# Hybrid residual block on one core: fill work ahead of the recurrence, transposes spread along the attention heads, two paired projection units turned into four single gates

## The chip, the core and the metric

The kernel runs on 1 core of one Trainium2 chip. Its time is the device time of one execution in microseconds. The median of 3 runs is 1808.64 us (1808.52 to 1810.89). All arithmetic is 32-bit: a large matrix product is done as three passes over operands that were split into a rounded high part and the rest (`h` and `l`), so that "a matmul of the program" is a group of three on TensorE at lines L115, L116 and L117 (helper `mm3`).

## The reference

One layer of a streaming encoder on x (1024 tokens x 1024 channels) and 256 memory tokens:

```
h = rmsnorm(x);  z = h @ w_in          # 2048 recurrence + 1544 forgetting attention + 512 memory + 3072 gate columns
y_a = gated linear recurrence          # 4 heads, 128x128 state, chunkwise: S = diag(f) S + (1-f) i^T, o = S^T q
y_b = forgetting attention             # 8 heads x 64, softmax(q k^T/8 + F_t - F_s), causal, 128-query blocks, normed q and k
y_c = cross-attention to the memory    # 4 heads x 128
merged = sum over 3 branches of sigmoid(gate_b) * (y_b @ w_b)
x = x + merged @ w_out
x = x + (gelu(conv3(h2 Wa)) * (h2 Wv)) @ w_down ,  h2 = rmsnorm(x)
```

## The kernel before, in words

The program is a chain of stages, and the order of each engine's instructions is fixed when the program is built: a scheduler runs a timeline of the whole program once and writes each engine's instructions down in the order in which that timeline starts them. On the chip every engine works through its list in that order. Three things steer the scheduler. `ahead(gen, 300)` gives a stage's instructions priority. `held(gen, lag)` lets a step of filling work start only behind the instruction that stands `lag` entries back in the list `state["at"]`, to which the recurrence and the attention add their matmuls as they go. `weave` interleaves two generators in proportion to their step counts.

The stages that matter here, with their place in the profiled span:

- 56 to 292 us, the projections that are done in pairs. `dense_unit` takes two 128-channel chunks of the input projection and computes them with seven block products instead of eight (four sums of the right-hand blocks, called T1 to T4, are made once by `differences`; L437 sums the weights). One unit is 7 products x 4 k-blocks x 3 passes = 84 matmuls of 512 columns. There are 11 units: 12 recurrence chunks, 4 memory-query chunks and 6 of the 24 gate chunks (`NPAIR` = 6).
- 292 to 400 us, recurrence values and `NMEM` = 2 single gates, woven with the memory attention. A single gate is `cm_chunk`: 2 halves x 8 k-blocks x 3 passes = 48 matmuls of 512 columns, so two gates take 96.
- 400 to 602 us, four recurrence heads (`hgrn_mix`), each in two halves, woven with a generator `fill` of 33 steps: 16 steps of attention values, one step for the forget-gate cumulative sum (L648 to L659), and 8 steps each of `fox_proj(0)` and `fox_proj(1)`, the query/key projections. A projection step is 8 k-blocks x 3 passes = 24 matmuls of 256 columns. `fox_proj(2)` follows at 602 to 624.
- 624 to 969 us, eight attention heads in four pairs (`fox_attn(p, i)`), woven with `fox_proj(3)` and then with the 12 remaining gates (`NFOX` lists the gates per head). `fox_prep(p)` loads the normed queries and keys of one pair (tile `zl`), transposes them on TensorE (L800, 16 transposes a pair) and spreads each transposed block over tiles `kh`, `kl`, `qa` by ScalarE, VectorE and GpSimd (L805 to L812). The preparation of pair p+1 is issued at the start of the second head of pair p, and its transposes may not start before the last score matmul (L839) of the head before.
- then the branch projections, the output projection, the ConvGLU.

In an attention head one query block goes: scores L838/L839 on TensorE, bias and row maximum on VectorE (L845), exponential on ScalarE (L855), normalising on GpSimd (L857), transposes L869 to L872, split L121/L129, values L881/L882.

## Time and profile before

| what | value |
|---|---|
| median of 3 runs | 1808.64 us |
| the profiled execution | 1810.57 us, its span 1808.8 us, mean granted TensorE clock 0.984 |
| busy share of the span | TensorE 97%, VectorE 67%, ScalarE 45%, GpSimd 17% |
| chain that ended last | TensorE 85%, VectorE 6%, DMA 3%, ScalarE 3% |
| DMA | 256.74 MB, mean 142 GB/s |

"Busy" on TensorE counts a matmul from its start to its modelled end, about 0.39 us for 512 columns, while the next one starts after about 0.23 us. So a price is best read from the starts of neighbouring rows in a timeline, or from a window that holds nothing else, not from the mean duration of a group.

### The profile page before, as it was taken

What the parts mean: (1) busy time and instruction counts of PE and PEld (TensorE: products, weight loads), DVE (VectorE), ACT (ScalarE), POOL (GpSimd) and SP (SyncE); (2) the same over time, 40 slices, a digit from 0 to 9 for tenths busy, and PEclk for the clock granted to TensorE, in tenths of its full rate; (3) what the DMA queues carried; (4) which work ended last, traced back from release to release, by engine and by line L of the source; (5) the groups of instructions that cost most, each with busy time, mean ns of one, the idle gap of its engine ahead of it and who ended that gap; (6) DMA issues with size and microseconds to landing.
All of it is one profiled execution on the core that took longest, in us unless ns stands there. A gap on an engine that the chain in (4) does not pass through costs nothing.

```text
span 1808.8 us, 24826 instructions
## 1 busy us (share of the span) xinstructions
PE 1748.3 (97%) x9021; PEld 1474.3 (82%) x9021; DVE 1207.3 (67%) x2215; ACT 815.9 (45%) x1436; POOL 312.8 (17%) x431
## 2 busy tenths in 40 slices
PE   8999999988989998999999999999999999999999
PEld 6778888967989986877888888878888888888887
DVE  7656665547878566666575665688787777766654
ACT  8634433646565354445452133544444334443332
POOL 1100000314334344333230000021111111100000
PEclk9999999998999998999999999999999999999999
DMA  9533323242221422312147463265545444395682
GB/s 354 175 121 105 97 95 129 83 148 87 94 70 59 165 75 80 108 65 88 55 154 258 146 216 116 98 193 146 150 148 145 130 150 134 111 340 191 227 289 82
DMA packets 97227, 256.74 MB, mean 142 GB/s; under 512 B 10816, under 2 KB 17736, under 8 KB 97104
## 3 DMA queue, kind: packets, MB, share of 16 engines
q1 hardware_dynamic: 77904, 186.46, 29.3%
q0 software_dynamic: 19200, 68.69, 13.1%
q8 instruction: 71, 1.16, 0.3%
q14 instruction: 52, 0.43, 0.1%
HBM read 195.56 MB, written 82.61 MB: 154 GB/s over the span
## 4 chain that ended last, share of the span: by engine, by line
PE 85%; DVE 6%; DMA 3%; ACT 3%; issue 2%; POOL 1%; SPq 0%; DVEq 0%; ACTq 0%; POOLq 0%
PE pp L116 18%; PE pp L117 18%; PE pp L115 18%; PE lg L117 5%; PE lg L115 5%; PE lg L116 5%; PE tr L116 2%; PE tr L115 2%; PE tr L117 2%; PE lg L1001 1%; PE po L882 1%; PE lg L838 1%; PE po L117 1%; PE po L115 1%; PE po L116 1%
## 5 line engine op out<-in xcount | busy, mean ns | idle before, releaser
L121 ACT CAST wh<-s 128x512 fp32r<-128x512 f32 x129 | 77.6, 619 | 174.3 <-PE pp L116 83.8
L115 PE MATMUL pp<-wh,uh 128*128 128x256 f32 (+1 forms) x512 | 149.2, 292 | 0.0
L117 PE MATMUL pp<-wh,ul 128*128 128x256 f32 (+1 forms) x512 | 148.1, 290 | 0.0
L116 PE MATMUL pp<-wl,uh 128*128 128x256 f32 (+1 forms) x512 | 148.1, 290 | 0.0
L115 PE MATMUL pp<-uh,wh 128*128 128x512 f32 x300 | 122.1, 407 | 0.0
L117 PE MATMUL pp<-uh,wl 128*128 128x512 f32 x300 | 121.4, 405 | 0.0
L116 PE MATMUL pp<-ul,wh 128*128 128x512 f32 x300 | 120.4, 401 | 0.0
L121 ACT CAST wh<-rw 128x512 fp32r<-128x512 f32 x99 | 60.3, 619 | 112.5 <-PE pp L116 67.4
L121 ACT CAST wh<-raw 128x1024 fp32r<-128x1024 f32 (+2 forms) x68 | 59.2, 871 | 95.0 <-PE pp L116 86.8
L115 PEld LDWEIGHTS pp<-wh,uh 128*128 128x128 f32 x512 | 99.1, 194 | 0.7
L116 PEld LDWEIGHTS pp<-wl,uh 128*128 128x128 f32 x512 | 98.7, 193 | 0.4
L117 PEld LDWEIGHTS pp<-wh,ul 128*128 128x128 f32 x512 | 98.7, 193 | 0.2
L1308 POOL DMA_DIRECT2D rw<-in_w_up x44 | 24.1, 555 | 428.1 <-ACT sqs L1243 197.4
L121 ACT CAST dwh<-wr 128x1024 fp32r<-128x1024 f32 (+1 forms) x41 | 40.1, 978 | 118.0 <-PE tr L116 38.1
L129 DVE TENSOR_TENSOR wl<-raw,wh 128x1024 fp32r<-128x1024 f32 (+2 forms) x67 | 71.1, 1062 | 23.3 <-ACT wh L121 22.8
L855 ACT ACTIVATE pt<-pt,st 128x128 f32<-128x128 f32 (+3 forms) x64 | 49.7, 777 | 50.1 <-DVE st L852 34.1
L129 DVE TENSOR_TENSOR dwl<-wr,dwh 128x1024 fp32r<-128x1024 f32 (+1 forms) x41 | 46.3, 1130 | 32.5 <-ACT dwh L121 32.5
L115 PEld LDWEIGHTS pp<-uh,wh 128*128 128x128 f32 x300 | 58.3, 194 | 12.0 <-ACT wh L121 0.3
L117 PEld LDWEIGHTS pp<-uh,wl 128*128 128x128 f32 x300 | 57.4, 191 | 12.3
L116 PEld LDWEIGHTS pp<-ul,wh 128*128 128x128 f32 x300 | 57.6, 192 | 11.4
L129 DVE TENSOR_TENSOR pl<-tr,ph 128x512 fp32r<-128x512 f32 (+1 forms) x80 | 49.9, 633 | 20.4 <-ACT ph L121 19.6
L857 POOL TENSOR_SCALAR pt<-pt,st 128x128 f32<-128x128 f32 (+3 forms) x64 | 48.5, 759 | 81.1 <-DVE st L856 55.1
(491 smaller groups left out, 5440.4 us busy)
## 6 DMA issues: line engine op xcount, KB each, us to landing
rw<-in_w_up POOLq DMA_DIRECT2D x44, 512.0 KB, 4.7
sd<-in_w_dn POOLq DMA_DIRECT2D x30, 512.0 KB, 6.0
br<-yd SPq DMA_DIRECT2D x30, 512.0 KB, 4.9
gd<-gt SPq DMA_DIRECT2D x48, 256.0 KB, 2.0
gt<-gd SPq DMA_DIRECT2D x48, 256.0 KB, 2.7
yd<-fc SPq DMA_DIRECT2D x44, 256.0 KB, 2.2
rw<-in_w_pair POOLq DMA_DIRECT2D x20, 512.0 KB, 5.5
wr<-sd SPq DMA_DIRECT2D x20, 512.0 KB, 4.6
```

Source lines behind the costliest of these rows:

```text
L115: PE.matmul(ps, lh, rh, start=first, stop=False, skip_group_check=more)
L116: PE.matmul(ps, lh, rl, start=False, stop=False, skip_group_check=more)
L117: PE.matmul(ps, ll, rh, start=False, stop=last, skip_group_check=more)
L121: return S.copy(out, in_)
L129: return (sub or V).tensor_sub(l, src, h.bitcast(F32))
L838: PE.matmul(ps[:, :w], qa[i][:, tsl], kh[i][:, s0:s0 + w], start=True, stop=False)
L855: S.activation(pt[:, :ns], pt[:, :ns], AF.Exp, bias=st[:, 2:3], accum_out=st[:, 3:4])
L857: late["pool"] = G.tensor_scalar(pt[:, :ns], pt[:, :ns], st[:, 3:4], 0.0, ALU.mult, ALU.add)
L882: late["pv"] = PE.matmul(o, vhl[:, sb, :], pl[:, src], start=False, stop=last)
L1001: mm = PE.matmul(o[:, b * 64:(b + 1) * 64], X[:, b * P:(b + 1) * P], Xq[:, b * bpb:(b + 1) * bpb, :], start=True, stop=True)
L1308: late["raw"] = G.dma_start(raw[:, 2 * i:2 * i + 2, :], src[:, 2 * i:2 * i + 2, :])
```

## The change

- `NPAIR` goes from 6 to 2: 9 paired units instead of 11. The four gates that drop out are computed as single gates in the attention heads: `NFOX` goes from 0,2,2,2,2,2,2,0 to 0,3,2,3,2,3,3,0.
- Five of the 33 steps of `fill` are issued ahead of the first recurrence head, without a hold; each head is then woven with 7 steps (before: 8, 8, 8, 9). The hold's lag is 4 instead of 3, and 10 in the attention heads.
- `fox_prep` becomes a generator: the preparation of the next pair is woven through the second head of each pair instead of standing at its start, with priority; its transposes no longer wait for the score matmul, and its two loads go to the projection's own buffers (`z`, 2 of them) instead of those of the attention weights (`pt`, 4). Three of the eight steps of `fox_proj(3)` come ahead of the first attention head.
- The vector operations that make T2 and T3 are issued behind T1's, without the wait for the first gates.
- The last of the recurrence's eight stores is issued by GpSimd instead of SyncE.

```diff
-NCOVER, NPAIR, NMEM = 2, 6, 2
-NFOX = [0, 2, 2, 2, 2, 2, 2, 0]
+NCOVER, NPAIR, NMEM = 2, 2, 2
+NFOX = [0, 3, 2, 3, 2, 3, 3, 0]
...
-LAG = 3
+LAG, FOX_LAG = 4, 10
...
             V.tensor_sub(b11, b11, b12)
             family_block("T1", k, b11)
+        for t1, b12, b21, b22 in b:
+            V.scalar_tensor_tensor(out=t1, in0=t1, scalar=-1.0, in1=b22, op0=ALU.mult, op1=ALU.subtract)
+            V.tensor_sub(b12, b22, b12)
         yield
         with tc.issue_after(first_gates.ins):
             for k, (t1, b12, b21, b22) in enumerate(b):
-                V.scalar_tensor_tensor(out=t1, in0=t1, scalar=-1.0, in1=b22, op0=ALU.mult, op1=ALU.subtract)
                 family_block("T2", k, t1)
...
             for k, (t2, b12, b21, b22) in enumerate(b):
-                V.tensor_sub(b12, b22, b12)
                 family_block("T3", k, b12)
...
-    def fox_prep(p, after=None):
-        zs = [pf.tile([P, 4, 256], F32, tag="pt", name=f"zl{p}_{n}", bufs=4) for n in range(2)]
+    def fox_prep(p):
+        zs = [z_tile(f"zl{p}_{n}") if p else pf.tile([P, 4, 256], F32, tag="pt", name=f"zl{p}_{n}", bufs=4)
+              for n in range(2)]
...
-                with tc.issue_after(after.ins) if after is not None else nullcontext():
-                    for b in range(4):
-                        PE.transpose(ptr[:, b * P:(b + 1) * P], z[:, b, what * P:(what + 1) * P], ident)
+                for b in range(4):
+                    PE.transpose(ptr[:, b * P:(b + 1) * P], z[:, b, what * P:(what + 1) * P], ident)
...
+                yield
...
-                SP.dma_start(yad[:, h, sl], yo)
+                (SP if h < 3 or n == 0 else G).dma_start(yad[:, h, sl], yo)
...
     fill = chain(fox_values(), fox_proj(0), fox_proj(1))
+    run_all(islice(fill, 5))
     for h in range(4):
-        weave((ahead(hgrn_mix(h), AHEAD), HGRN_STEPS), (held(islice(fill, 8 + (h == 3))), 8))
+        weave((ahead(hgrn_mix(h), AHEAD), HGRN_STEPS), (held(islice(fill, 7)), 7))
...
-    fox_prep(0)
+    run_all(fox_prep(0))
+    rest = fox_proj(3)
+    run_all(islice(rest, 3))
     for p in range(4):
         for i in range(2 if p < 3 else 1):
-            if i:
-                fox_prep(p + 1, fox_sets[p][3])
             count = NFOX[2 * p + i]
             weave((ahead(fox_attn(p, i), AHEAD), FOX_STEPS),
-                  (held(gates_early(count) if p + i else fox_proj(3)), 2 * count if p + i else 8))
+                  (ahead(fox_prep(p + 1), AHEAD) if i else iter(()), 4),
+                  (held(gates_early(count) if p + i else rest, FOX_LAG), 2 * count if p + i else 5))
```

Three places show what the change does to the built order. Lines of the changed kernel lie 1 to 3 below those of the one before (L838 becomes L841, L800 L803, L951 L954).

TensorE where the memory attention ends (`po<-mph`) and the first recurrence head begins (`lg<-qq,kt`). Before:

```order
L117 MATMUL pp<-uh_85,wl 128x512
L115 MATMUL po<-mph,mvh 128x512
L116 MATMUL po<-mpl,mvh 128x512
L117 MATMUL po<-mph,mvl 128x512
L951 MATMUL lg<-qq,kt 128x192 x4
L115 MATMUL pp<-wh,uh_71 128x256
```

Now the same place has 120 matmuls of the attention-value projection (`pp<-wh,uh`, 256 columns) in it; its first rows, where they begin among the last matmuls of the memory attention:

```order
L115 MATMUL po<-mph,mvh 128x512
L115 MATMUL pp<-wh,uh_77 128x256
L116 MATMUL po<-mpl,mvh 128x512
L117 MATMUL po<-mph,mvl 128x512
L115 MATMUL po<-mph,mvh 128x512
L116 MATMUL po<-mpl,mvh 128x512
L117 MATMUL po<-mph,mvl 128x512
L116 MATMUL pp<-wl,uh_77 128x256
L117 MATMUL pp<-wh,ul_78 128x256
```

All five steps stand in TensorE's list before the recurrence's first matmul; 110 of the 120 rows stand behind the last one of the memory attention.

TensorE at the start of the fourth attention head (second head of pair 1), where the transposes of pair 2 (`tr<-ident,zl`) are. Before, the last three groups of four stand close together:

```order
L800 MATMUL tr<-ident,zl_0_7434 128x128 x4
L115 MATMUL pp<-uh_83,wh 128x512
L116 MATMUL pp<-ul_84,wh 128x512
L117 MATMUL pp<-uh_83,wl 128x512
L115 MATMUL pp<-uh_85,wh 128x512
L116 MATMUL pp<-ul_86,wh 128x512
L117 MATMUL pp<-uh_85,wl 128x512
L800 MATMUL tr<-ident,zl_1_7435 128x128 x4
L838 MATMUL lg<-kh_1_6585,qa_1_6587 128x512
L839 MATMUL lg<-kl_1_6589,qa_1_6587 128x512
L800 MATMUL tr<-ident,zl_1_7435 128x128 x4
L869 MATMUL tr<-ident,pt 128x128
```

Now the second group alternates with the attention's own transposes, and the third and fourth come 56 and 119 rows behind it:

```order
L885 MATMUL po<-pl,vhl 128x128
L803 MATMUL tr<-ident,zl_0_7227 128x128
L872 MATMUL tr<-ident,pt 128x128
L803 MATMUL tr<-ident,zl_0_7227 128x128
L873 MATMUL tr<-ident,pt 128x128
L803 MATMUL tr<-ident,zl_0_7227 128x128
L872 MATMUL tr<-ident,pt 128x128
L803 MATMUL tr<-ident,zl_0_7227 128x128
L873 MATMUL tr<-ident,pt 128x128
L117 MATMUL pp<-uh_81,wl 128x512
```

The order also deals the gates differently: in the third and the fifth head (two gates each) it has 103 and 104 gate matmuls, none of them after about two thirds of the head's score matmuls (before: 99 and 89, spread over the whole head); the heads with three gates have 129 to 137.

VectorE around the first gates (`gt<-..,rx`), where the differences for T2 and T3 (`xk<-xk,xk`) are made. Before:

```order
L129 TENSOR_TENSOR T1l<-xk_98,T1h 128x512
L384 TENSOR_TENSOR gt<-lg,rx 128x512 x2
L384 TENSOR_TENSOR gt<-pp,rx 128x512
L129 TENSOR_TENSOR wl<-s_729,wh 128x512
L129 TENSOR_TENSOR wl<-s_735,wh 128x512
L384 TENSOR_TENSOR gt<-po,rx 128x512
L564 SCALAR_TENSOR_TENSOR xk_95<-xk_95,xk_99 128x512
L564 SCALAR_TENSOR_TENSOR xk_96<-xk_96,xk_100 128x512
```

Now:

```order
L129 TENSOR_TENSOR T1l<-xk_98,T1h 128x512
L562 SCALAR_TENSOR_TENSOR xk_96<-xk_96,xk_100 128x512
L562 SCALAR_TENSOR_TENSOR xk_97<-xk_97,xk_101 128x512
L574 SCALAR_TENSOR_TENSOR t4s_516<-xk_95,xk_99 128x512
L562 SCALAR_TENSOR_TENSOR xk_98<-xk_98,xk_102 128x512
L574 SCALAR_TENSOR_TENSOR t4s_517<-xk_96,xk_100 128x512
L574 SCALAR_TENSOR_TENSOR t4ta<-xk_97,xk_101 128x512
L574 SCALAR_TENSOR_TENSOR t4tb<-xk_98,xk_102 128x512
L129 TENSOR_TENSOR wl<-s_733,wh 128x512
L129 TENSOR_TENSOR wl<-s_739,wh 128x512
L384 TENSOR_TENSOR gt<-lg,rx 128x512 x2
L384 TENSOR_TENSOR gt<-pp,rx 128x512
```

All twelve differences, T4's four among them, now stand ahead of the first gates in VectorE's list.

More of the change, by code (lines that the diff above doesn't have):

```diff
@@ L791, in fox_prep @@
         kl = [pf.tile([P, T], F32R, tag=f"kl{i}", name=f"kl{i}_{p}", bufs=1 + i) for i in range(2)]
+        fox_sets[p] = [kh, kl, qa, None, pools["vf"]]
         for n in range(2):
@@ L813, in fox_prep @@
                                                in1=qa[i][a, sl].bitcast(F32), op0=ALU.mult, op1=ALU.subtract)
-        fox_sets[p] = [kh, kl, qa, None, pools["vf"]]
+                yield
     def fox_attn(p, i):
@@ L1045, in hgrn_mix, with finish @@
                     St = Sn
-            def finish(po=po, gz=gz, sl=sl):
+            def finish(po=po, gz=gz, sl=sl, n=n):
                 o2 = ph.tile([P, 4, P], F32, tag="o2", name="o2")
```

## The prediction

> **What bounds the kernel now.** I read the page first, then windows over the stages that the change touches, then timelines at the places where TensorE waits.
>
> ```profile
> PE 1748.3 (97%) x9021; PEld 1474.3 (82%) x9021; DVE 1207.3 (67%) x2215; ACT 815.9 (45%) x1436; POOL 312.8 (17%) x431
> PE 85%; DVE 6%; DMA 3%; ACT 3%; issue 2%; POOL 1%; SPq 0%; DVEq 0%; ACTq 0%; POOLq 0%
> ```
>
> TensorE is 85% of the chain that ended last. The stages differ, and the second view, windows (span, then busy time and count of each engine; the last three columns are the granted clock, the DMA share and GB/s), shows where it is not full:
>
> ```profile
> 241.54:280.60 39.06, 39.06 (x170) 31.55 (x169) 24.07 (x40) 15.75 (x29) 1.05 (x2) 1.00 0.24 81
> 399.50:414.50 15.00, 0.02 (x1) 0.02 (x1) 8.12 (x13) 6.31 (x14) 3.39 (x4) 0.61 0.90 330
> 414.50:435.00 20.50, 19.79 (x144) 19.07 (x145) 15.40 (x32) 15.28 (x39) 7.84 (x9) 0.87 0.07 28
> 500.30:529.30 29.00, 23.93 (x174) 22.48 (x173) 21.75 (x45) 19.16 (x46) 12.13 (x11) 0.88 0.21 65
> 529.30:550.10 20.80, 20.80 (x179) 20.22 (x178) 18.39 (x38) 11.31 (x33) 8.27 (x8) 1.00 0.13 39
> 550.10:571.20 21.10, 21.10 (x181) 20.59 (x180) 19.28 (x39) 13.40 (x33) 10.90 (x10) 1.00 0.24 89
> 624.00:657.00 33.00, 26.31 (x168) 24.14 (x167) 25.80 (x75) 17.57 (x35) 18.02 (x25) 0.84 0.23 78
> 657.00:707.00 50.00, 44.48 (x276) 39.32 (x275) 34.29 (x90) 27.64 (x51) 22.42 (x27) 0.90 0.28 96
> 707.00:745.00 38.00, 36.80 (x202) 30.95 (x201) 21.77 (x74) 16.96 (x36) 10.22 (x17) 1.00 0.23 78
> 745.00:791.50 46.50, 42.57 (x221) 35.41 (x220) 28.78 (x87) 22.89 (x44) 15.59 (x25) 0.93 0.29 101
> 791.50:827.40 35.90, 34.50 (x191) 29.04 (x190) 22.19 (x75) 17.24 (x36) 10.32 (x17) 1.00 0.19 62
> 827.40:873.70 46.30, 42.38 (x220) 35.45 (x219) 28.21 (x87) 22.90 (x44) 15.57 (x25) 0.93 0.27 89
> 873.70:908.80 35.10, 34.47 (x191) 28.98 (x190) 21.41 (x77) 16.62 (x37) 10.30 (x17) 1.00 0.20 64
> sum 319.00, PE 294.97 PEld 251.25 DVE 205.55 ACT 160.14 POOL 113.06; mean PE 36.87 PEld 31.41 DVE 25.69 ACT 20.02 POOL 14.13
> ```
>
> The first row is two paired units: TensorE full, nothing to hide there. The second is an empty gap of 15.00 us ahead of the recurrence. The next four are halves of recurrence heads: full, except 500 to 529. From 624 on come the attention heads, one row each; the sum row has all eight windows (the eighth ends at 943). The second heads of the pairs (745, 827) take 46 us, the first heads (791, 874) 35 to 36.
>
> **The paired units.** Two units go. A full window of two is 39.06 us, so the term is **-39.1 us**, bare TensorE time.
>
> **The four gates.** A gate is 48 matmuls of 512 columns. Three starts in a row:
>
> ```profile
> 760.59 0.39 PE L115 MATMUL pp<-uh,wh 128*128 128x512 f32 x1
> 760.82 0.40 PE L116 MATMUL pp<-ul,wh 128*128 128x512 f32 x1
> 761.05 0.40 PE L117 MATMUL pp<-uh,wl 128*128 128x512 f32 x1
> ```
>
> They lie 0.23 us apart; the two units give 39.06/168 = 0.2325 us. 4 x 48 x 0.2325 = **+44.6 us** of TensorE work. So TensorE has 5.5 us more to do than before, and every microsecond of gain has to come out of time in which it now waits or runs cold. The gates' casts and products on ScalarE and VectorE are hidden: in the window at 745 these have 23 and 29 us of work in 46.5. Without that cover a gate's own vector work (a 1024-wide split and two products) would add under 3 us.
>
> **Slack in the attention heads.** Over the eight windows idle time is 319.00 - 294.97 = 24.0 us; the clock below 1.00 costs at most 0.16 x 33 + 0.10 x 50 + 0.07 x 46.5 + 0.07 x 46.3 = 16.8 us. Together 40.8 us is the most that can be won, 0 the least. What of it the change reaches:
>
> ```profile
> 631.04 0.30 PE L838 MATMUL lg<-kh,qa 128*128 128x128 f32 x1 [3.11 <-DVE qa L812]
> 632.07 0.41 PE L117 MATMUL pp<-wh,ul 128*128 128x256 f32 x1
> 632.29 0.41 PE L115 MATMUL pp<-wh,uh 128*128 128x256 f32 x1
> 769.05 0.63 PE L800 MATMUL tr<-ident,zl 128*128 128x128 f32 x4 [2.47 <-DVE qa L812]
> 770.44 0.30 PE L869 MATMUL tr<-ident,pt 128*128 128x128 f32 x1 [0.76 <-DVE kl L806]
>   DVE qa L812: 6.1, 3
> ```
>
> At 631 TensorE waits 3.11 us for the first pair's preparation and then runs cold (0.21 us between 256-column matmuls that lie 0.119 apart when warm, as quoted further down), some 1.5 us more. With three projection steps ahead that is filled: 5 us. The last row is from the transposes' own view: three waits for VectorE's `qa`, 6.1 us in all, one per preparation of a next pair; 769.05 is one of them. What such a preparation costs in all is the difference between a second and a first head. The gate matmuls in these two windows, by the tiles that they read (`uh`, then `ul`):
>
> ```profile
> 791.50:827.40 35.90, 20.40 (x60) 1.00 0.19 62
> 827.40:873.70 46.30, 24.15 (x69) 0.93 0.27 89
> 791.50:827.40 35.90, 11.69 (x30) 1.00 0.19 62
> 827.40:873.70 46.30, 14.16 (x35) 0.93 0.27 89
> ```
>
> 104 against 90 gate matmuls: 14 x 0.2325 = 3.3 us of the difference of 10.4. The 16 transposes are 16 x 0.09 (the four at 758.75, below, free TensorE after 0.36) = 1.5. The remaining 5.6 us is stall, three times over: 16.8.
>
> ```profile
> 758.75 0.60 PE L800 MATMUL tr<-ident,zl 128*128 128x128 f32 x4
> 759.11 0.48 PE L115 MATMUL pp<-uh,wh 128*128 128x512 f32 x1
> ```
>
> Spreading the groups gives VectorE, ScalarE and GpSimd time between two of them, and the third gate of a second head stands beside them as cover; the 3 loads, 16 transposes and 24 casts of a pair remain. I count 5 + 16.8 = 21.8 as won, 4 us elsewhere from the longer lag (fill may start ten entries behind the attention, so it is at hand when a score waits), and take 6 back: in the third and fifth heads the order has no gate left for the last third, where the attention alone sets the pace. **-20 us**, half of what there is.
>
> **The gap ahead of the recurrence.** It is a chain that no fill was allowed into:
>
> ```profile
> 397.92 1.08 ACT L121 CAST wh<-raw 128x1056 fp32r<-128x1056 f32 x1 [1.99 <-PE pp L116]
> 402.56 6.07 DMA ha<-hd
> 414.51 2.90 PE L951 MATMUL lg<-qq,kt 128*128 128x192 f32 x8 [14.99 <-DVE qq L943]
> 603.20 0.27 PE L115 MATMUL pp<-wh,uh 128*128 128x256 f32 x1
> 603.32 0.28 PE L116 MATMUL pp<-wl,uh 128*128 128x256 f32 x1
> 603.43 0.28 PE L117 MATMUL pp<-wh,ul 128*128 128x256 f32 x1
> ```
>
> The head waits for its own load (6.07 us), logarithm and scan. Five steps are 5 x 24 x 0.119 = 14.3 us and fit. Their weights are there: at 397.92 ScalarE already casts a 1056-wide piece, the second part of the value projection, so the first is ready. The gap itself does not get shorter; the heads do, if TensorE sets their pace: 14.3/8 = 1.8 us a half. In the full halves VectorE has 18.39 of 20.80 and 19.28 of 21.10 us, so 2.4 and 1.8 us is all the room there is, and a bound that close is not reached. I take two thirds: **-9.5 us**. Bounds: 0, if VectorE's chain sets the halves; -17, if all 14.3 come and the lost clock at 414 (0.13 x 20.5 = 2.7) too. The half at 500 with its 5 us of idle moves to another place and stays.
>
> The page "TensorE: Matmul & The Clock Gate" of the Trainium skill (Part 1: The HAM clock gate) says that an idle window of about 3.4 us halves TensorE's clock until it has been busy as long again; by it a filled gap saves about 1.7 us, an estimate from its figures. The clock of 0.61 and 0.87 at the gap agrees in kind; the term above doesn't use it.
>
> **The differences T2 and T3.** In the first unit TensorE waits 0.68 and 0.58 us while VectorE stood idle earlier:
>
> ```profile
> 66.59 1.29 DVE L384 TENSOR_TENSOR gt<-lg,rx 128x512 f32<-128x512 f32 x2 [4.00 <-DMA rx<-rx_d]
> 87.26 0.51 PE L115 MATMUL pp<-T2h,wh 128*128 128x512 f32 x1 [0.68 <-ACT fe L430]
> 91.94 0.50 PE L117 MATMUL lg<-uh,wl 128*128 128x512 f32 x1 [0.58 <-DVE wl L129]
> ```
>
> Four idle microseconds take six of the twelve operations at 0.65 us (two take 1.29 in the first row); the others may push the first gates back by up to 3.9 us, which must not hold a PSUM bank that TensorE wants. **-0.8 us**, between -1.3 and +1.5. The store moved to GpSimd is one issue there, with 18 of 33 us busy: nothing.
>
> **Sum**: -39.1 + 44.6 - 20 - 9.5 - 0.8 = -24.8. The profiled execution took 1810.57 us (span 1808.8 and 1.8 around it), 1.9 above the median of 1808.64. So 1785.8 for such an execution, **1784 us** for the median, 1.4% less. About 0.2% (3.6 us) is what a measurement of this kernel can tell from no change.
>
> **Rivals.** *More is won.* Spread preparation and more fill leave only 11 us of the attention's slack, and the halves shrink by nearly all they can: -39.1 + 44.6 - 30 - 13 - 0.8 = -38.3, 1770 us. For it: first heads, full of gates, keep a clock of 1.00. Against it: the attention's own chain remains.
>
> *The gates only cost what they cost.* The preparation's stall goes elsewhere, nothing of the slack is filled, and VectorE holds the recurrence: -39.1 + 44.6 - 4 - 0.8 = +0.7, 1809 us. For it: VectorE's 92% in the halves. Against: the named waits are TensorE's own, with fill standing behind them.
>
> *Slower.* Ten entries of lag let the fixed order put long blocks of gates ahead of scores: in the second to seventh heads the order has a block of 35 to 61 gate matmuls between two neighbouring pairs of scores (24 at most before). 61 are 14 us in which VectorE, ScalarE and GpSimd run dry, and behind them a last third without cover. At 3 us for each of six heads on top of the case above: 1827 us. It decides as soon as the attention chain alone, from a pair's scores to its values, is longer than the fill left behind it. The same page of the Trainium skill (Part 2: What happens when you issue a matmul) says that matmuls stay in program order and only weight loads move ahead; by it such a block really stands in the way, which 770.44 above, a transpose queued behind the preparation's, bears out in the small.
>
> *The early fill isn't ready.* If a step in the gap waits for its buffers, the head queues behind it and the 9.5 us are gone: 1794 us. The cast at 397.92 speaks against it.
>
> **Chances.** Forecast 0.63, more won 0.15, cost only 0.10, slower 0.07, not ready 0.05. The forecast's own range, with its two slack terms 40% larger or smaller (12 us), is 1772 to 1796. Reaching to the cases on both sides so that about 2 in 10 stay out gives 1764 to 1803. Faster: 0.63 + 0.15 + 0.05 and a third of the third case, 0.86; same 0.06; slower 0.08.
>
> **What would show it.** Right: nine units of 19.5 us; TensorE busy from 399 to 414 with a clock of 1.00; halves of 19 to 20 us; no wait of transposes for `qa`; second heads of 49 to 53 us with three gates at a clock of 0.97 or more; the seventh head at 44 to 47. Wrong: halves still above 20.5 us (VectorE's bound); second heads of 55 or more; idle time in the third and fifth heads' last third above 5 us each; a T2 wait above 2 us.

## The result and the profile after

The changed kernel takes 1793.12 us (median; 1789.67 to 1793.96), the kernel before 1808.58 in the same comparison: a ratio of 0.991 with a 95% interval of 0.9893 to 0.9927. It is faster by 15.5 us, where 24.6 were forecast, and lies in the range. The profiled execution took 1793.35 us, its span 1791.6, 17.2 less than the span of before.

The page of after, the lines on busy time and on the chain that ended last:

```profile
PE 1744.6 (97%) x9045; PEld 1475.5 (82%) x9045; DVE 1190.9 (66%) x2191; ACT 808.9 (45%) x1420; POOL 318.8 (18%) x428
PE 90%; DVE 4%; ACT 2%; DMA 2%; issue 2%; POOL 1%; SPq 0%; DVEq 0%; ACTq 0%; POOLq 0%
```

TensorE's share of the chain went from 85% to 90%, and VectorE's from 6% to 4%. By stages, from the starts that the timelines give, the span changed like this:

| stage | before | after | difference | forecast |
|---|---|---|---|---|
| start to the first score of the recurrence | 414.5 | 384.0 | -30.5 | -39.1 - 0.8 |
| recurrence with `fox_proj(2)` (to 624.0 and 593.5) | 209.5 | 209.5 | 0.0 | -9.5 |
| attention with `fox_proj(3)`, to the branch projections | 356.6 | 370.7 | +14.1 | +44.6 - 20 |
| the rest | 828.2 | 827.4 | -0.8 | 0 |

The attention is counted from the first transposes of its preparation (`tr<-ident,zl`) on, which stand at 624.0 before and at 593.5 now. (The expectations further down put the recurrence of after at 206.4 us and the growth of the attention at 17.2; they are 209.5 and 14.1.) So the attention came out better than forecast, the recurrence and the stage ahead of it worse. Windows over the recurrence of after: the gap ahead of it, four of its halves, the last half, and `fox_proj(2)`:

```profile
368.90:384.00 15.10, 13.18 (x112) 12.99 (x110) 7.32 (x12) 8.11 (x17) 3.00 (x4) 1.00 0.99 352
404.80:424.80 20.00, 18.15 (x151) 17.36 (x150) 16.07 (x39) 10.04 (x21) 8.47 (x8) 0.99 0.32 103
424.80:447.60 22.80, 22.80 (x182) 22.40 (x182) 17.44 (x41) 13.69 (x40) 9.20 (x10) 0.93 0.17 59
447.60:471.40 23.80, 18.57 (x144) 16.83 (x142) 20.71 (x41) 17.66 (x33) 8.35 (x9) 0.94 0.38 123
493.70:515.90 22.20, 18.26 (x161) 17.75 (x159) 21.13 (x42) 13.16 (x32) 11.38 (x11) 0.94 0.30 108
538.90:572.00 33.10, 27.24 (x212) 26.23 (x212) 23.44 (x49) 12.72 (x26) 13.02 (x10) 0.90 0.23 88
572.00:593.50 21.50, 21.50 (x185) 21.50 (x184) 5.68 (x8) 6.47 (x13) 7.21 (x6) 1.00 0.46 162
```

The gap is filled as foreseen (13.18 of 15.10 us busy, clock 1.00, before 0.02 and 0.61). But the halves behind it still take 20 to 24 us, with TensorE idle for up to 5 us and, but for the first two, at a clock of 0.90 to 0.94. What was taken out of them came back as waiting, as the whole stage shows, before and after:

```profile
414.50:624.00 209.50, 202.20 (x1652) 196.19 (x1653) 155.91 (x320) 116.61 (x272) 80.86 (x77) 0.97 0.24 80
384.00:593.50 209.50, 190.47 (x1533) 184.54 (x1534) 155.42 (x322) 114.85 (x268) 83.96 (x78) 0.94 0.23 81
```

Some 120 matmuls fewer, the same 209.5 us: idle time went from 7.3 to 19.0 us.

The attention heads of after, the second to the sixth, and the sum of the eight windows from 593.50 to 932.20:

```profile
625.10:674.00 48.90, 47.88 (x260) 40.34 (x259) 33.50 (x97) 26.31 (x51) 20.10 (x26) 1.00 0.38 131
674.00:712.30 38.30, 37.07 (x204) 31.24 (x202) 23.50 (x71) 17.82 (x35) 10.91 (x18) 1.00 0.28 95
712.30:761.00 48.70, 48.31 (x250) 40.89 (x251) 29.21 (x93) 24.08 (x47) 17.80 (x26) 0.96 0.28 97
761.00:800.40 39.40, 38.13 (x207) 31.83 (x207) 23.08 (x70) 17.68 (x35) 9.93 (x16) 1.00 0.27 94
800.40:851.90 51.50, 48.53 (x253) 40.74 (x253) 30.66 (x95) 26.59 (x52) 17.80 (x27) 0.97 0.20 69
sum 338.70, PE 331.52 PEld 283.79 DVE 214.54 ACT 171.02 POOL 118.25; mean PE 41.44 PEld 35.47 DVE 26.82 ACT 21.38 POOL 14.78
```

Idle time is 338.70 - 331.52 = 7.2 us, before 24.0; the clock is 1.00 but for two heads at 0.96 and 0.97.

**Where 9 us went.** The first T2 product starts at 96.67 us, before at 87.26. The timelines of after between 66 and 91 us, GpSimd's loads, VectorE's product for the fourth gate tile, and TensorE:

```profile
66.59 2.25 POOL L463 DMA_DIRECT2D rw<-in_w_pair  x4 [10.45 <-DVE t4s L574]
77.51 0.69 DVE L384 TENSOR_TENSOR gt<-po,rx 128x512 f32<-128x512 f32 x1 [7.13 <-DMA gd<-gt]
83.67 0.79 PE L115 MATMUL pp<-uh,wh 128*128 128x512 f32 x1 [5.72 <-DVE gt L384]
84.26 0.63 PE L116 MATMUL pp<-ul,wh 128*128 128x512 f32 x1
84.69 0.63 PE L117 MATMUL pp<-uh,wl 128*128 128x512 f32 x1
90.09 0.39 PE L115 MATMUL pp<-uh,wh 128*128 128x512 f32 x1
90.31 0.40 PE L116 MATMUL pp<-ul,wh 128*128 128x512 f32 x1
```

and from the chain of waits in the same stretch, the store of the first gate tile from issue to landing:

```profile
69.88 7.54 DMA gd<-gt
```

The same places of before:

```profile
79.21 1.10 POOL L463 DMA_DIRECT2D rw<-in_w_pair  x2 [22.48 <-ACT gt L385]
70.74 0.69 DVE L384 TENSOR_TENSOR gt<-po,rx 128x512 f32<-128x512 f32 x1 [1.06 <-DMA gd<-gt]
gd<-gt SPq DMA_DIRECT2D x48, 256.0 KB, 2.0
```

The reading: T4's differences (L574, the last operations that read `xk`, the blocks of which all four sums are made) can only follow T2's and T3's. With these early, they too ran early, the storage of these blocks came free, and the four 512 KB weight loads of the next two units, whose tiles lie in it, started at 66.59 us instead of 79.21. They met the stores of the first gate tiles. The first store took 7.54 us (median of all such stores before: 2.0), and there are only three gate tiles, so the fourth product waited 7.13 us for it. The T2 and T3 splits and the next products, one of which frees the bank `pp`, stand behind it on VectorE; TensorE waited 5.72 us for that bank and then ran at one matmul per 0.43 us instead of 0.23 until 90.09. This is a reading of one trace; the first experiments test it.

### The profile page after: what moved, and what is told of

It is laid out like the page before. It is cut to its first block, busy times and chain, and to the rows that moved or that the text cites. A ratio compares the mean times of both kernels' runs of the same rounds, so it can differ in the third digit from the quotient of the medians.

```text
span 1791.6 us, 24844 instructions
## 1 busy us (share of the span) xinstructions
PE 1744.6 (97%) x9045; PEld 1475.5 (82%) x9045; DVE 1190.9 (66%) x2191; ACT 808.9 (45%) x1420; POOL 318.8 (18%) x428
## 4 chain that ended last, share of the span: by engine, by line
PE 90%; DVE 4%; ACT 2%; DMA 2%; issue 2%; POOL 1%; SPq 0%; DVEq 0%; ACTq 0%; POOLq 0%
PE pp L116 19%; PE pp L117 19%; PE pp L115 19%; PE lg L116 4%; PE lg L115 4%; PE lg L117 4%; PE tr L116 2%; PE tr L117 2%; PE tr L115 2%; PE po L885 1%; PE po L884 1%; PE lg L1004 1%; PE po L117 1%; PE po L115 1%; PE po L116 1%
## 5 line engine op out<-in xcount | busy, mean ns | idle before, releaser
L121 ACT CAST wh<-s 128x512 fp32r<-128x512 f32 x121 | 72.8, 619 | 171.9 <-PE pp L116 91.5
L115 PE MATMUL pp<-uh,wh 128*128 128x512 f32 x356 | 143.6, 404 | 6.7 <-DVE gt L384 5.7
L117 PE MATMUL pp<-uh,wl 128*128 128x512 f32 x356 | 144.2, 405 | 0.0
L116 PE MATMUL pp<-ul,wh 128*128 128x512 f32 x356 | 143.5, 403 | 0.0
L121 ACT CAST wh<-raw 128x1024 fp32r<-128x1024 f32 (+2 forms) x72 | 63.4, 880 | 93.1 <-PE pp L116 83.6
L115 PEld LDWEIGHTS pp<-uh,wh 128*128 128x128 f32 x356 | 68.7, 193 | 21.2 <-DVE gt L384 6.2
L116 PEld LDWEIGHTS pp<-ul,wh 128*128 128x128 f32 x356 | 68.4, 192 | 13.8
L117 PEld LDWEIGHTS pp<-uh,wl 128*128 128x128 f32 x356 | 68.3, 192 | 13.8
L121 ACT CAST ph<-tr 128x512 fp32r<-128x512 f32 (+1 forms) x80 | 42.3, 542 | 63.1 <-PE tr L873 29.6
```

Of the source, the lines that this page charges most:

```text
L115: PE.matmul(ps, lh, rh, start=first, stop=False, skip_group_check=more)
L116: PE.matmul(ps, lh, rl, start=False, stop=False, skip_group_check=more)
L117: PE.matmul(ps, ll, rh, start=False, stop=last, skip_group_check=more)
L121: return S.copy(out, in_)
```

## The experiments

Differences are between medians. The kernel before measured 1808.6 to 1811.1 us in the several comparisons, so 3 us between two of them say little; the ratio to before of the same comparison is given beside each. Unless said, all parts not named are those of the changed kernel, and every kernel computes the whole block.

| kernel | median us | ratio, 95% interval | to first recurrence score | to the attention's first transposes | to branch projections | rest |
|---|---|---|---|---|---|---|
| before | 1808.58 | 1 | 414.5 | 209.5 | 356.6 | 828.2 |
| after | 1793.12 | 0.991 [0.9893, 0.9927] | 384.0 | 209.5 | 370.7 | 827.4 |
| e1 differences back | 1779.78 | 0.9829 [0.9815, 0.9844] | 375.9 | 205.5 | 370.1 | 827.5 |
| e2 loads held in the order | 1790.14 | 0.9891 [0.9876, 0.9906] | 381.8 | 207.6 | 370.8 | 827.5 |
| e3 no fill ahead | 1782.42 | 0.9847 [0.9831, 0.9864] | 381.7 | 205.7 | 364.0 | 827.9 |
| e4 eleven units | 1801.07 | 0.9947 [0.9932, 0.9961] | 424.4 | 202.3 | 345.1 | 828.5 |
| f1 loads made to wait | 1783.37 | 0.9854 [0.9838, 0.9871] | 377.0 | 209.7 | 367.3 | 827.3 |
| f2 both undone (e1 and e3) | 1779.65 | 0.9834 [0.9819, 0.9848] | 374.5 | 205.5 | 370.2 | 827.4 |
| f3 f2, recurrence lag 3 | 1786.29 | 0.987 [0.9855, 0.9884] | 374.2 | 207.6 | 373.8 | 827.7 |
| f4 f2, attention lag 4 | 1772.38 | 0.9793 [0.9779, 0.9808] | 373.7 | 207.0 | 364.4 | 826.9 |
| g1 f4, preparation in one piece | 1786.61 | 0.9869 [0.9851, 0.9887] | 374.3 | 207.0 | 371.9 | 834.0 |
| g2 f4, fill ahead again | 1773.70 | 0.9794 [0.9774, 0.9814] | 375.7 | 205.4 | 364.9 | 826.8 |
| g3 f4, ten units | 1781.06 | 0.9837 [0.9820, 0.9854] | 394.7 | 207.3 | 352.1 | 826.8 |
| g4 before, fill ahead alone | 1799.40 | 0.9936 [0.9920, 0.9952] | 415.3 | 200.8 | 352.4 | 829.1 |

The last four columns are stage lengths in the profiled execution, read from the first row of each stage in TensorE's timeline. The attention's first transposes, and not its first score, are the border, because 60 or more rows of `fox_proj(3)` stand ahead of that score in all kernels but before and g4, which have 24 there.

### The early differences: e1, e2, f1

The first edit puts the eight differences of T2 and T3 back (T4's four can only follow them; the twelve of the expectation are counted with these):

```
-        for t1, b12, b21, b22 in b:
-            V.scalar_tensor_tensor(out=t1, ...)      # T2
-            V.tensor_sub(b12, b22, b12)              # T3
         yield
         with tc.issue_after(first_gates.ins):
             for k, (t1, b12, b21, b22) in enumerate(b):
+                V.scalar_tensor_tensor(out=t1, ...)
                 family_block("T2", k, t1)
```

(and likewise for T3).

> The changed kernel with one part undone: the twelve differences for T2 and T3 stand again inside their own steps, as in the kernel before; all else as changed. Theory A (mine, from the trace of after): made early, the differences free the halves of the first unit's sources, so the weight loads of the paired units start at 66.6 us instead of 79.2, collide with the stores of the gates' tiles, and the first T2 block starts 9.4 us later (87.3 to 96.7). By it the paired units end 7 to 9 us earlier: 1785 us (1784 to 1787). Theory B (the prediction's term of -0.8): the late start has another cause and the early differences save their waits: 1794 us, the same as after or a little more.

Measured: 1779.78 us, 13.3 less than after. The loads and T2 are back at their old places:

```profile
78.98 1.10 POOL L463 DMA_DIRECT2D rw<-in_w_pair  x2 [22.98 <-ACT gt L385]
87.03 0.51 PE L115 MATMUL pp<-T2h,wh 128*128 128x512 f32 x1 [0.68 <-ACT fe L430]
```

Theory A holds for the first stage (-8.1 us up to the recurrence); of the other 4 to 5 us, 4.0 lie in the recurrence, whose code is the same, which theory A had not foreseen. Its built order is not the same: 273 of the 1532 rows of TensorE in that stage stand at another place than in after (more on that at the fill ahead). The second edit was to tell the collision from the place of the vector work, by holding the loads back in the built order:

```
-            G.dma_start(t, src[:, 2 * i:2 * i + 2, :])
+            with nullcontext() if first else tc.issue_after(first_gates.ins):
+                G.dma_start(t, src[:, 2 * i:2 * i + 2, :])
```

> The changed kernel with the differences early, as changed, but the weight loads of the second and later paired units issued only behind the fourth of the first gates. It tells the collision of transfers from the mere place of the vector operations. If the loads that start early and collide with the gates' stores cost the time, 1785 to 1787 us, as with the differences put back, and the gate's store lands in about 2 us again instead of 7.5. If it is the place of the twelve operations on VectorE, ahead of the gates' first product, the time stays at 1793 us. If the later loads are themselves late for the second unit, a new wait of TensorE for cast weights shows up and the time lies above 1793.

Measured: 1790.14 us, but it tells nothing apart. The hold moves an instruction in the scheduler's timeline; on the chip the loads had nothing to wait for and GpSimd issued them even earlier. From the timeline and the chain of waits of this run:

```profile
65.31 2.24 POOL L464 DMA_DIRECT2D rw<-in_w_pair  x4 [10.46 <-DVE t4s L575]
69.56 6.78 DMA gd<-gt
```

TensorE's rows are the same as in after, one by one, through the whole program, and the 3 us between the two times are within what separates two comparisons. So the loads got something real to wait for: a write of 128 x 4 zeros into each of the two tiles, by VectorE behind the fourth gate's product.

```
         whole = None if first else dense.raw()
+        if held_units and not first:      # the first two later units
+            held_units.pop()
+            with tc.issue_after(first_gates.ins):
+                V.memset(whole[:, :, 0:1], 0.0)
```

> The changed kernel with the differences early, as changed, but the weight tiles of the second and third paired unit are first written with a zero (128 x 4 elements) by VectorE behind the fourth gate's product, so that their loads have something to wait for on the chip and cannot start before it. (In the run with loads held in the built order alone they still started at 65.3 us, so it told nothing of the collision.) If the early loads, colliding with the stores of the gates' tiles, are what holds the fourth tile back, the store lands in 2 to 3 us, the wait of 5.7 us at 83.7 and the cold stretch behind it go, T2 starts at 87 to 89 us and the time is 1780 to 1785 us. If the place of the twelve operations costs the time, the wait stays and the time is 1790 to 1794 us. If the loads then come too late for the second unit, TensorE waits for its weights between 100 and 125 us and the time lies between.

Measured: 1783.37 us, 9.7 less than after, with the differences still early. VectorE's and TensorE's rows at the places where after waits 7.13 and 5.72 us:

```profile
73.36 0.69 DVE L384 TENSOR_TENSOR gt<-po,rx 128x512 f32<-128x512 f32 x1 [1.61 <-DMA gd<-gt]
79.52 0.50 PE L115 MATMUL pp<-uh,wh 128*128 128x512 f32 x1 [0.23 <-DVE gt L384]
81.25 2.14 POOL L468 DMA_DIRECT2D rw<-in_w_pair  x4 [23.59 <-ACT gt L385]
```

T2 starts at 89.7 us. Here too TensorE's order is that of after, row by row. Of the gain 7.0 us lie ahead of the recurrence, none in it (209.7 against 209.5), and 3.4 in the attention, at a clock of 1.00 instead of 0.99: so up to 3.4 us of a stage can change with no change of the order in it. The place of the vector operations is not the cause of these 7.0 us; the loads that they let start are. That the loads slow the store by sharing the 16 DMA engines with it is the likely way (the DMA share was 0.96 between 70 and 74 us, 0.56 before), but the run shows only that the wait goes when they come later.

### The fill ahead of the recurrence: e3, g4, f2, g2, f3

```
-    run_all(islice(fill, 5))
     for h in range(4):
-        weave((ahead(hgrn_mix(h), AHEAD), HGRN_STEPS), (held(islice(fill, 7)), 7))
+        weave((ahead(hgrn_mix(h), AHEAD), HGRN_STEPS), (held(islice(fill, 8 + (h == 3))), 8))
```

> The changed kernel without the five steps ahead of the recurrence's first head: the 33 steps are dealt along the four heads again as 8, 8, 8 and 9; the lag of 4 and all else as changed. By the prediction's term the fill ahead is worth 9.5 us: 1802.6 us. Theory A, from the traces (the recurrence with what is issued behind it is 209.5 us before and 206.4 after, at clocks of 0.90 to 0.94 in the later halves): the work taken out of the heads is mostly given back as waits and lost clock, so it is worth 2 to 4 us: 1795 to 1797 us. Theory B: the lag of 4 instead of 3 eats part of it, and the fill ahead alone is worth the full 9 us or more: 1802 us or above.

Measured: 1782.42 us: without the five steps it is 10.7 us faster. Neither theory had this. The same edit the other way round, made alone on the kernel before:

```
+    run_all(islice(fill, 5))
...
-        weave((ahead(hgrn_mix(h), AHEAD), HGRN_STEPS), (held(islice(fill, 8 + (h == 3))), 8))
+        weave((ahead(hgrn_mix(h), AHEAD), HGRN_STEPS), (held(islice(fill, 7)), 7))
```

> The kernel before with one part of the change alone: five of the 33 fill steps ahead of the first recurrence head, 7 steps in each head. The lag stays 3, the rest as before. The prediction's term makes it 9.5 us faster: 1800 us against some 1810 of the same chip. Theory A (the halves are set by the recurrence's own chain): no gain from the work taken out, 1806 to 1814 us, with halves of 20 to 24 us as before.

Measured: 1799.40 us against 1810.0, 10.6 us faster, which is the prediction's number and against theory A. With both parts undone:

> The changed kernel without two of its parts: the differences back at their old place, and no fill ahead of the recurrence. Undone one at a time these gave 13.3 and 10.7 us. Theory A: two mechanisms at different places, so they add up: 1767 to 1771 us. Theory B: part of each gain is the order that the scheduler happens to write for the recurrence and the attention heads once its timeline is shifted (in the trace without the fill ahead 6.2 of the 12.3 us lie behind the first attention head, which that edit does not touch), so they do not add: 1773 to 1779 us.

Measured: 1779.65 us, the same as with the differences alone put back: theory B went in the right direction, and on this footing the five steps are worth nothing. And once more, with a lag of 4 in the attention (that run follows below):

> As the kernel with the differences put back and a lag of 4 in the attention heads, with the five steps ahead of the recurrence as changed (the kernel without them: 1772.4 us). With the differences early the five steps cost 10.7 us, with the differences put back they cost nothing (1779.78 against 1779.65). Theory A: the recurrence's halves are set by its own chain of VectorE, ScalarE and GpSimd, so taking 14.3 us of TensorE work out of them wins nothing by itself, and the rest is the order that falls out: 1770 to 1777 us. The prediction's term of -9.5 would make it 1763 us.

Measured: 1773.70 us against 1772.38, nothing again. One edit, four footings: -10.6, +0.1 and +1.3 (nothing both times), +10.7 us. In the recurrence it is -8.7, 0.0, -1.6 and +3.8 us. The first of these footings also has a lag of 3 where the others have 4; whether that matters for the fill ahead was not run. To see what the 14.3 us of TensorE work do to the halves, here is one window from the first half's start to the last half's, of before, after, the kernel before with fill ahead, and after without it:

```profile
414.50:571.20 156.70, 149.53 (x1205) 144.30 (x1206) 127.08 (x267) 97.06 (x235) 62.72 (x63) 0.96 0.20 67
```

```profile
384.00:538.90 154.90, 141.72 (x1141) 136.81 (x1142) 126.29 (x267) 95.67 (x230) 63.73 (x63) 0.94 0.20 68
```

```profile
415.30:567.30 152.00, 141.29 (x1132) 135.78 (x1133) 126.01 (x268) 94.97 (x229) 65.83 (x63) 0.96 0.22 70
```

```profile
381.70:533.60 151.90, 146.17 (x1213) 141.52 (x1214) 126.09 (x266) 95.39 (x232) 69.47 (x64) 0.99 0.22 70
```

With 33 steps in the heads TensorE has 1205 and 1213 matmuls there, with 28 steps 1141 and 1132, and the time does not follow them. Over all the kernels of this study these seven halves took 151.9 to 156.7 us with 33 steps (seven kernels) and 152.0 to 156.7 with 28 (seven kernels): the same span of values. Over the whole stage of the table, TensorE's idle time is 5.7 to 7.5 us in the kernels with 33 steps and 11.9 to 19.0 in those with 28, while the stage takes 207.1 and 205.8 us in the mean. So TensorE's work does not set the halves; what is taken out of them turns into idle time and lost clock. VectorE is busy for 126 to 127 of these 152 to 157 us in all four, so it is not full throughout either, though it has 21.13 of 22.20 us in the half at 493.70 of after. A chain across engines is left. TensorE's waits for it in after name VectorE's `A` tiles (L1000 and L1009), 10.6 us in the seven halves; no run here changed that chain.

What then moves the time by 10 us either way? The span without the fill ahead is 12.3 us shorter than that of after, and this lies in three stages: 2.3 ahead of the recurrence, 3.8 in it, 6.7 in the attention (and 0.5 lost behind). The first belongs to the edit: on all four footings the stage ahead is longer with the fill, by 0.8 to 2.3 us, because the last matmul of the memory attention comes that much later; in after, 10 of the 120 rows stand in front of it. The gap behind it stays at 15 us. The third is not touched by the edit, but the scheduler writes the order from one timeline, and a shift in the recurrence changes the order of gates and scores later: 464 of the 2016 rows of TensorE in the attention stand at another place than in after. In the same way the last half fell out badly in after: fill ran out, TensorE was busy for 27.24 of 33.1 us at a clock of 0.90, while with the differences put back, and the same generator, it was this:

```profile
532.60:565.00 32.40, 30.39 (x256) 29.27 (x256) 23.06 (x46) 14.54 (x32) 11.79 (x9) 1.00 0.31 100
```

256 matmuls against 212 in a shorter window. Where the order differs, stages that the edit does not touch differ by 3.6 to 6.7 us here, of which up to 3.4 us can come with the same order, as f1 has shown. Which rows of the order cost the rest is left open. The recurrence's lag alone, back to 3 on the kernel with both parts undone:

```
-LAG, FOX_LAG = 4, 10
+LAG, FOX_LAG = 3, 10
```

> As the kernel with both parts undone, but the recurrence's hold has its lag of 3 back. From first score to first attention score the recurrence took 216.5 us before, and 213.7 without the fill ahead with 8.6 us more of TensorE work in it; the half with 5 us of idle time is gone there. Theory A: the lag of 4 did this (fill that may start one entry earlier is at hand when a difference or an exponential is late): with 3 it is 4 to 10 us slower than with both undone. Theory B: it is the order as it falls, and the lag is worth nothing by itself: within 3 us of it, on either side.

Measured: 1786.29 us, 6.6 slower, inside theory A's range, yet by the table only 2.1 us of it lie in the recurrence and 3.6 in the attention, whose lag was not changed. So this is no proof for the lag: it is the size of what a shifted order does.

### The attention: e4, f4, g1, g3

```
-NCOVER, NPAIR, NMEM = 2, 2, 2
-NFOX = [0, 3, 2, 3, 2, 3, 3, 0]
+NCOVER, NPAIR, NMEM = 2, 6, 2
+NFOX = [0, 2, 2, 2, 2, 2, 2, 0]
```

> The changed kernel with the four gates and the two units put back: six paired units more than the first five, as before, and two gates in each of the second to seventh attention heads. Everything else as changed. The two units are worth +39.1 us. By the prediction the four gates cost 44.6 us of TensorE work of which some goes into slack; the attention stage grew by 17.2 us with them and would have shrunk without. If the dealt transposes and the longer lag alone (without more gates) won 12 to 20 us in the attention stage, the time is 1793 + 39 - 44.6 + what the gates filled, that is 1793 to 1802 us. If the third gates are what fills the slack, and the deal alone wins little, the stage stays near its 356.6 us of before and the time is 1793 + 39 - 17 = 1815 us.

Measured: 1801.07 us, 8.0 slower than after. The attention is 25.6 us shorter without the four gates (345.1 against 370.7): of their 44.6 us of work 19 fell into slack. The time lies in the first of the two ranges, in which the dealing and the longer lag were to win 12 to 20 us of the attention. It is 11.5 us shorter than before with the same 12 gates, but 9.2 of these lie in the first two heads (73.8 us against 83.0), where the projection steps ahead of the first head fill its wait too. The six other heads, up to the branch projections, take 271.3 us against 273.6. What these parts won is more in the clock (0.98, before 0.95) than in the idle time:

```profile
626.70:971.80 345.10, 325.79 (x1825) 276.68 (x1824) 222.20 (x667) 172.72 (x337) 122.69 (x176) 0.98 0.35 115
```

TensorE is idle for 19.3 us, against 24.0 before and 7.2 in after. It is the third gates that fill most of the idle time.

The lag in the attention heads, from 10 to 4, on the kernel with both parts undone:

```
-LAG, FOX_LAG = 4, 10
+LAG, FOX_LAG = 4, 4
```

> As the kernel with both parts undone, but the hold in the attention heads has a lag of 4 instead of 10. The prediction counts 4 us for the longer lag, so 4 us slower. Rival: ten entries of lag put blocks of up to 61 gate matmuls ahead of scores and leave the last third of a head without fill; a lag of 4 spreads them, and the time is the same or 2 to 6 us less. If the fill is what the second heads need while their transposes run, a short lag costs more than the prediction says, 8 to 15 us.

Measured: 1772.38 us, 7.3 less: the rival's direction, a little more than its size. The windows of the fourth, fifth and sixth head with a lag of 10, then with a lag of 4:

```profile
698.90:746.00 47.10, 46.75 (x250) 39.61 (x251) 29.17 (x93) 24.08 (x47) 17.70 (x26) 1.00 0.31 101
746.00:785.40 39.40, 38.12 (x207) 31.82 (x206) 23.07 (x70) 17.73 (x35) 9.90 (x16) 1.00 0.27 93
785.40:837.70 52.30, 49.52 (x254) 41.63 (x254) 30.55 (x95) 26.42 (x52) 17.77 (x27) 0.93 0.22 69
```

```profile
698.40:738.50 40.10, 40.05 (x219) 33.85 (x219) 26.03 (x83) 21.58 (x42) 15.71 (x24) 1.00 0.28 94
738.50:782.50 44.00, 44.00 (x243) 37.56 (x242) 27.31 (x83) 21.07 (x41) 12.86 (x19) 1.00 0.27 95
782.50:822.50 40.00, 39.95 (x219) 33.82 (x218) 25.93 (x83) 21.57 (x42) 15.69 (x24) 1.00 0.24 81
```

With the short lag the heads are even, 40 and 44 us, TensorE does not wait (0.05 us a head at most) and stays at a clock of 1.00. Ten entries of lag put too many gates into the second heads, where the sixth then has 2.8 us of idle time at a clock of 0.93. This kernel, at 0.9793 of before, is faster than before and after.

On it, the preparation in one piece again:

```
+            if i:
+                run_all(fox_prep(p + 1, fox_sets[p][3]))
             weave((ahead(fox_attn(p, i), AHEAD), FOX_STEPS),
-                  (ahead(fox_prep(p + 1), AHEAD) if i else iter(()), 4),
```

(with the transposes behind `after` again, in the built order).

> As the kernel with both parts undone and a lag of 4 in the attention heads (1772.4 us), but the preparation of the next pair stands again in one piece at the start of the second head, its transposes behind the last score of the head before in the built order. The third gates and all else stay. The prediction counts 16.8 us of stall for three such preparations, gone with the dealing: by it 1787 to 1790 us, with waits of the transposes for qa of 2 us each back. Rival: the third gates and the order around them are what filled the stall, the dealing adds little: 1772 to 1778 us.

Measured: 1786.61 us, 14.2 slower, near the prediction's 16.8. But the place is only half the one that was foreseen: 7.5 us are in the attention, with no wait of the transposes for `qa`, and 7.1 in the rest. There TensorE waits twice for a merged tile at the start of the branch projections:

```profile
955.86 0.50 PE L115 MATMUL pp<-ych,wh 128*128 128x512 f32 x1 [1.77 <-DVE mg L1145]
958.28 0.47 PE L115 MATMUL pp<-ych,wh 128*128 128x512 f32 x1 [1.46 <-DVE mg L1145]
```

Why the merge is late in this order is not settled. 1275 of the 2016 rows of TensorE in the attention stand at another place than in f4, so part of the 14.2 us can be the order too.

Last, two of the four gates back into a unit:

```
-NCOVER, NPAIR, NMEM = 2, 2, 2
-NFOX = [0, 3, 2, 3, 2, 3, 3, 0]
+NCOVER, NPAIR, NMEM = 2, 4, 2
+NFOX = [0, 2, 2, 3, 2, 3, 2, 0]
```

> As the kernel with both parts undone and a lag of 4 in the attention heads (1772.4 us, attention windows with 2.3 us of idle time in 316), but two of the four gates go back into a paired unit: ten units, 14 gates in the heads. A unit costs 19.5 us, two gates 22.3. If the heads are full either way, TensorE's work alone decides: 2.8 us less, 1769.6 us. If the third gates are what fills the heads, the two taken out leave idle time behind: at 3 us for each of the two heads, 1775 us or more; if all of their work fell into slack, 1790 us.

Measured: 1781.06 us, 8.7 slower. The stage ahead is 21.0 longer, the attention 12.3 shorter: two gates of 22.3 us cost 12.3. The second head of this kernel, with two gates instead of three, shows what they had filled:

```profile
631.80:673.60 41.80, 37.22 (x201) 30.70 (x200) 30.83 (x93) 24.95 (x47) 20.39 (x26) 0.92 0.38 121
```

4.6 us of idle time at a clock of 0.92; with three gates that head takes 43.9 us and does 35 more matmuls.

## Why the prediction was right or wrong

**The two units, -39.1:** right. With the collision gone the first stage is 38.6 (e1) and 40.0 us (f2) shorter than before.

**The differences T2 and T3, -0.8 between -1.3 and +1.5:** wrong, and the miss that no other one cancels. It measured +7.0 (f1) to +8.1 us (e1) up to the recurrence, and 13.3 in the time with what the shifted order brought. What is left of that stage's shortfall (-30.5 in place of -39.9) fits the 0.8 to 2.3 us that the fill ahead adds there. Nor did the saving of 0.8 us show: with the loads made to wait the stage is still 1.1 us longer than with the differences put back. The prediction asked whether the early operations would push the first gates back and hold a PSUM bank. It named the right victim, but not the way: it didn't ask what else the operations release. The last reader of a buffer moved forward, the loads that wait for the buffer moved with it, and they hit stores that three gate tiles cannot wait for. So the sign that was set, a T2 wait above 2 us, did not come: T2's first product at 96.67 us has no wait before it, and the 5.72 us stand ahead of it, at a gate's product.

**The gap, -9.5 between 0 and -17:** wrong; it came out at its bound of 0. The recurrence stage takes 209.5 us before and after. The gap was filled as said, but "the heads do, if TensorE sets their pace" failed: it does not, as the fourteen kernels' halves show. The sign that the prediction had set for this ("halves still above 20.5 us") came up. Its reason, VectorE's bound, is not shown: VectorE has 126 of 152 us, though in one half 21.13 of 22.20. On the kernel before the same edit gives -10.6, 8.7 of it in the recurrence, as the term said; why there and on none of the three other footings is open.

**Four gates +44.6, slack -20:** right in kind, 10.5 us too cautious. The stage grew by 14.1, so 30.5 of the 40.8 us of slack were won. By parts: the dealing was put at 16.8 and measured 14.2 with a lag of 4, but only 7.5 of it in the attention and none as the wait for `qa` that was named, so that the two sizes agree by luck; the gates as cover are worth more than thought (two cost 12.3 of 22.3, and without the third gates 19.3 us of idle time stay); the longer lag was put at -4 and is +7.3, the wrong sign; the first head's 5 us were won (window 593.50 to 625.10: 0.28 us idle).

**The sum.** -24.8 was forecast for the span, -17.2 came: +9.4 from the first stage, +9.5 from the recurrence, -10.5 from the attention, -0.8 from the rest. The misses in the recurrence and in the attention cancel, which is luck; the one in the first stage is what is left. With all three of one sign the time would have been outside the range.

**The rivals.** "Slower" had its mechanism right, blocks of gates that ten entries of lag put ahead of the scores, but it is worth 7.3 us, not 18, and didn't decide. "The early fill isn't ready" is out (13.18 of 15.10 us busy, clock 1.00), though its 1794 us is the time that came. "The gates only cost what they cost" is out for the gates; that the recurrence gets no shorter, its other half, came true. "More is won", 1770 us, is about what the changed kernel gives with its differences put back and a lag of 4 in the attention (1772.38).

**What was to show it.** TensorE busy in the gap: yes. Second heads of 49 to 53 us with a clock of 0.97 or more: 48.9, 48.7, 51.5 at 1.00, 0.96, 0.97. No wait of transposes for `qa`: none is left. The seventh head, 44 to 47: 43.5. Halves of 19 to 20: no, 20 to 24. Units of 19.5: yes, after the first two. Idle time in the third and fifth heads above 5 us: no, 1.2 and 1.3.

## What to carry to other kernels

When an operation is moved forward, list not only what it delays but what it releases: if it is the last reader of a buffer, the transfers into that buffer start earlier too, and must be set against what else uses the DMA engines then. A hold in the built order holds nothing on the chip unless a dependency stands behind it. Where one timeline decides the whole order, an edit's worth belongs to its footing (here -10.6 to +10.7 us for the same five steps), so price it as a stage's own change plus a few us of order either way, and try it again after the others are in.

## What was not expected of the hardware

- A store of 256 KB that lands in 2.0 us (median of 48) took 7.54 us with four loads of 512 KB issued 3.3 us ahead of it on another queue, and about 2 with the loads made to wait (issued at 71.25 us, the product that waits for it at 73.36).
- After 5.72 us without work TensorE ran at 0.43 us a 512-column matmul and came back to 0.23 at 90.09 us, 6.4 us after its restart; these 15 matmuls took 6.42 us where 15 x 0.2325 are 3.5, so 2.9 us on top of the wait. The page "TensorE: Matmul & The Clock Gate" of the Trainium skill (Part 1: The HAM clock gate) puts the halving after an idle window of about 3.4 us, which agrees, and the return after a busy window of the same length; the 6.4 us measured are nearly two of these, which its free-running window allows. That rule alone does not cover this trace: TensorE also ran at a clock of 0.50 from 424.5 to 427.8 us and from 714.6 to 717.8, and the longest waits just ahead of these were 1.52 us (up to 423.79) and 1.28 (up to 712.35).
- A stretch can count as fully busy and still be slow: 22.80 of 22.80 us at a clock of 0.93 in the half at 424.80. The clock column has to be read beside the busy one.
